# A two-layer hybrid trunk: where the constant tiles start, and corrections of attention scores over 64 or 128 rows of the array

## The chip, the cores and the metric

The kernel runs on one core of a Trainium2 chip. The metric is the time of one execution on the device in microseconds (us). Three runs of the kernel before gave 1586.66, 1589.82 and 1590.9 us; the median is 1589.82.

The engines of the core have short names in the profile: PE is TensorE's matmul, PEld its weight load, DVE is VectorE, ACT is ScalarE, POOL is GpSimd, SP is SyncE, which issues most of the transfers.

## The reference

Two layers over 512 positions of width 1024, all in float32. Each layer normalises x, projects it, mixes the positions in three ways side by side, adds the result to x, and then applies a gated feed-forward part with a short convolution. The part of the attention that the change touches:

```python
q = rmsnorm(da_q.reshape(B, S, DA_HEADS, 2, DA_QK_DIM), da_q_norm_g[l]) * (DA_QK_DIM ** -0.5)
k = rmsnorm(da_k.reshape(B, S, DA_HEADS, 2, DA_QK_DIM), da_k_norm_g[l])
...
s = jnp.einsum('bhmqd,bhmkd->bhmqk', qb, kh) + bias[None, :, None]
s = jnp.where(dist >= 0, s, neg)
p = jax.nn.softmax(s, axis=-1)
a = p[:, :, 0] - lam * p[:, :, 1]
return jnp.einsum('bhqk,bhke->bhqe', a, vh)
```

There are 4 heads, each with two maps (index m) of 64 features. The rest of a layer is retention over 4 heads, a short convolution, three gates of width 1024, an output projection, and the feed-forward part of width 2816.

## The kernel before, in words

**Exact products from two parts.** A float32 operand is held as two float32r tiles: the rounded value (hi) and what rounding left (lo). `mm3` (L145 to L149) multiplies hi by hi, hi by lo and lo by hi into one accumulator, so every product of the reference is three matmuls. The rows of the profile at L147, L148 and L149 are these three. `T.matmul(o, a, b)` lets `b` stream through the array while `a` stands in it as 128x128 weights; the profile names the streaming operand first.

**Work by position and by feature.** x lies transposed, in eight tiles of 128 features by 512 positions. `split_x` (L239) makes the two parts of each, times a gain. `natural` (L301) projects with x standing and the weights streaming, for what is wanted by position: the retention's queries, keys, values and gate (512 columns) and the heads (384 columns). `project` (L265) has the weights standing and x streaming, 512 columns: the convolution's inputs and gates (`proj_T`) and the feed-forward gate and up tiles (pg and pu). The branches (pb), the output projection (po) and the down projection (p2) stream other tiles: the mixers' outputs (om), the gated sum (y), the activations (act).

**Weights.** SyncE loads a weight tile, ScalarE rounds it (L138), VectorE subtracts (L139). Three pairs of these tiles take turns.

**The attention.** For each head `attention` (L425) turns queries and keys by transposes. Map m sits in rows 0 to 63 or 64 to 127. `qs2[:, m]` holds the hi part of a map's queries in the map's own half of the rows and the lo part in the other half; `kh2[:, m]` holds the hi part of the keys in both halves. One matmul over 128 rows (L462) gives hi times hi and lo times hi. What is missing, hi queries by lo keys, is the score correction (L465): the lo keys of both maps share one tile `kl` (L446, map 0 in its upper half, map 1 in its lower), and each correction is a matmul over the 64 rows of its map. A block of 128 queries has 128, 256, 384 or 512 keys, by the causal mask, so each head has four blocks with two maps: eight matmuls at L462 and eight at L465.

**Order.** `staggered` runs the heads and the retention in steps side by side, `weave` puts projections that do not depend on them between the steps, and a scheduler with its own estimate of durations settles the final order on each engine. On TensorE the two maps' matmuls of a block stand next to each other or with projection matmuls between them.

**Where tiles start.** A pool lays out its tiles one after the other in each partition, each rounded up to 32 bytes. The pool `cp` of constants comes first. It begins with two tiles of 512 bytes, a tile of 4 bytes (`warm`) and two of 560; x follows, 288 bytes past a multiple of 512, then the tables, then state, qz and the parts of x, all 480 bytes past a multiple of 512 (that is 32 past a multiple of 64). The pools `wp` (weights) and `tp` (om, y, act, queries, keys) come behind it, and in the kernel before their large tiles start on multiples of 2048.

Of the kernel before, what the change touches and what calls it, by code (L numbers as in the profile page):

```python
# [20 lines left out]
P = 128  # L21
D = 1024
S = 512
# [14 lines left out]
SINGLE = 1  # L38
SOME = 5
# [4 lines left out]
# columns of the packed per-layer parameters  # L44
# [5 lines left out]
def trunk(ctx, tc, xT, wr, wh, wt, wda, wret, wsc, wo, wf, w2, par, lamp, relb, onehot, mask, rope, gtab, out):  # L50
# [30 lines left out]
    def weave(first, second):  # L81
        """Steps of first, each followed by about COVER us of second."""
        due = 0.0
        for _ in first:
            due += COVER
            while due > 0.0:
                cost = next(second, None)
                if cost is None:
                    break
                due -= cost  # L90
        run(second)

    def staggered(tasks):
        """Tasks side by side, a step of each at a time, each from its own start on."""
        t = 0
        while tasks:
            live = []
            for start, task in tasks:
                if start <= t and next(task, DONE) is DONE:
                    continue  # L100
                live.append((start, task))
            tasks = live
            t += 1
            yield
# [12 lines left out]
    def ordered(i):  # L117
        """The program's first loads follow one another as they are written."""
        if starting[0]:
            tc.keep_in_program_order(i)  # L120
        return i
# [23 lines left out]
    def mm3(o, a, b, start, stop):  # L145
        """o += a.T @ b in float32, from operands in two exact parts."""
        T.matmul(o, a[0], b[0], start=start, stop=False)  # L147
        T.matmul(o, a[0], b[1], start=False, stop=False)  # L148
        T.matmul(o, a[1], b[0], start=False, stop=stop)  # L149

    def split(src, hi, lo, g=None):
        """float32 src (times a column) as two float32r parts."""
        if g is None:
            A.copy(hi, src)
            V.tensor_tensor(lo, src, hi.bitcast(F32), ALU.subtract)
        else:
            A.activation(hi, src, AF.Copy, scale=g)
            V.scalar_tensor_tensor(lo, src, g, hi.bitcast(F32), ALU.mult, ALU.subtract)
        return hi, lo
# [6 lines left out]
    ident = cp.tile([P, P], F32, name="ident")  # L166
    make_identity(nc, ident)
    ones = cp.tile([P, P], F32, name="ones")
    G.memset(ones, 1.0)
    warm = cp.tile([P, 1], F32, name="warm")  # L170
    A.activation(warm, ones[:, 0:1], AF.Tanh)
    # the array's clock rises with use: bring it up while the first loads are under way
# [7 lines left out]
    x = [cp.tile([P, S], F32, name=f"x{k}") for k in range(KT)]  # L180
# [5 lines left out]
    rope_t = cp.tile([P, 2, ST, 64], F32, name="rope_t")  # L186
    gtab_t = cp.tile([P, ST, 8], F32, name="gtab_t")
    mask_t = cp.tile([P, P], F32, name="mask_t")
    bias_t = cp.tile([P, H, S], F32, name="bias_t")
# [8 lines left out]
    def biases():  # L198
        """The negated relative bias, with the causal mask, as a Toeplitz tile per head."""
        rb = cp.tile([BUCKETS + 1, H], F32, name="rb")  # L200
        V.memset(rb[BUCKETS : BUCKETS + 1], -BIG)
        G.dma_start(rb[:BUCKETS], relb)
        line = dr.tile([H, 640], F32, name="line")
        for a, b in ((0, 512), (512, 640)):
            oh = temp(f"oh{a}", b - a)[: BUCKETS + 1]
            G.dma_start(oh, onehot[:, a:b])
            ps = aux(f"psb{a}")
            T.matmul(ps[:H, : b - a], rb, oh, start=True, stop=True)
            row = temp(f"line{a}", b - a)[:H]
            V.tensor_copy(row, ps[:H, : b - a])  # L210
            G.dma_start(line[:, a:b], row)
        skew = dr.tile([H, P * 640], F32, name="skew")
        G.dma_start(skew.rearrange("h (p n) -> h p n", n=640), line.unsqueeze(1).broadcast_to([H, P, 640]))
        src = skew[:, 127 : 127 + 639 * P].rearrange("h (p n) -> p h n", n=639)
        G.dma_start(bias_t, src[:, :, :S])

    # zero columns in front of what the convolutions read
# [4 lines left out]
    # the retention's states and queries of two heads, on the diagonal blocks  # L222
    state = cp.tile([P, 2, ST - 1, P], F32R, name="state")
    G.memset(state.bitcast(F32), 0.0)
    qz = [cp.tile([P, ST, 2, P], F32R, name=f"qz{a}") for a in range(2)]
# [3 lines left out]
    def rsqrt(f, v, n, name):  # L229
        """v ** -0.5: a first guess from the exponent, and Newton's steps to float32's last bit."""  # L230
        t = sp.tile([P, n], F32, tag=f"nt{n}", name=f"nt{name}", bufs=2)
        V.tensor_scalar(t.bitcast(I32), v.bitcast(I32), 1, None, ALU.logical_shift_right)
        V.tensor_scalar(f.bitcast(I32), t.bitcast(I32), -1.0, float(0x5F3759DF), ALU.mult, ALU.add)
        for _ in range(3):
            V.scalar_tensor_tensor(t, f, -0.5, f, ALU.mult, ALU.mult)
            V.tensor_tensor(t, t, v, ALU.mult)
            V.scalar_tensor_tensor(f, t, 1.5, f, ALU.add, ALU.mult)

    def split_x(l, which, name, k):  # L239
        """x times its gain in two parts."""  # L240
        hi = cp.tile([P, S], F32R, tag=f"xh{k}", name=f"xh{k}_{name}")
        lo = cp.tile([P, S], F32R, tag=f"xl{k}", name=f"xl{k}_{name}")
        return split(x[k], hi, lo, pars[l][:, which + k : which + k + 1])

    def norm_x(name):
        """1 / rms of x by column and by row."""
# [18 lines left out]
    def project(xg, ps, w):  # L265
        """ps[e, s] = sum over d of w[d, e] x[d, s], for 128 columns of a weight."""
        for k, xk in enumerate(xg):
            sl = slice(k * P, (k + 1) * P)
            mm3(ps, (w[0][:, sl], w[1][:, sl]), xk, k == 0, k == len(xg) - 1)

    def rms_cols(sq, n, scale, name):
        """(mean square + eps) ** -0.5 over the last axis of sq [p, n, d]."""
# [7 lines left out]
    def transposes(src, name):  # L280
        """Four 128 x 128 blocks of src(st), side by side in a bank."""
# [10 lines left out]
    def layer(l):  # L292
# [8 lines left out]
        def natural(src, w, name, evacuate):  # L301
            """w columns of the input projection by position, one bank per 128 positions; in steps."""
# [70 lines left out]
        # -lambda, in every partition  # L373
# [23 lines left out]
        def head_chunk(h):  # L397
            """Head h of the attention: queries and keys by position, values in two parts."""
# [26 lines left out]
        def attention(h):  # L425
            """A head in steps: scores and softmax of a block of queries, the difference of its two
            maps, its transpose, its product with the values; neighbouring blocks overlap."""
# [3 lines left out]
            # a map's queries in two parts above each other, against keys whose first part stands twice  # L431
# [3 lines left out]
            kl = tp.tile([P, S], F32R, tag="kl", name=f"kl{h}{L}", bufs=2)  # L435
# [6 lines left out]
            for m in range(2):  # L442
# [3 lines left out]
                V.scalar_tensor_tensor(kl[a], ps[a], gk[a], kh2[a, m].bitcast(F32), ALU.mult, ALU.subtract)  # L446
# [7 lines left out]
            def scores(i):  # L454
# [8 lines left out]
                for m in range(2):  # L463
                    # a map in either half of the array's rows
                    T.matmul(pS2[m][:, :W], qs2[halves[m], m, qs], kl[halves[m], :W], start=False, stop=True)  # L465
# [8 lines left out]
            def combine(i):  # L474
                # e0 / z0 - lambda e1 / z1, times z0
# [15 lines left out]
            def values(i):  # L491
                # against both parts of v at once, side by side
# [41 lines left out]
        kn = (wide(f"knh{L}"), wide(f"knl{L}"))  # L534

        def retention(p):
# [34 lines left out]
            def scores(b):  # L571
                # two blocks of positions, both heads
# [97 lines left out]
        def side(b, src, mats):  # L670
            """The gated sum over the short convolution (b = 2) and the retention (b = 1)."""
# [12 lines left out]
        # the retention and the heads, with what does not depend on them between their steps  # L684
# [73 lines left out]
def _consts():  # L758
    """Tables that depend on the shapes alone."""
# [18 lines left out]
    # the retention's decay between positions i and j, g ** i for queries, g ** -j / 8 for keys  # L778
# [11 lines left out]
def _layout(i):  # L790
    """The inputs as the program's tensors: tiles of weights that are contiguous by partition."""
    C = np.ascontiguousarray

    def cols(w, n):
        # [L, K*P, n*P] -> [L, n, P, K*P]
        L, kk, _ = w.shape
        return C(w.reshape(L, kk // P, P, n, P).transpose(0, 3, 2, 1, 4)).reshape(L, n, P, kk)
# [4 lines left out]
    def rows(w, n, width):  # L802
        # two rows of tiles beside each other
        return C(w.reshape(DEPTH, 4, 2, P, n, width).transpose(0, 4, 1, 3, 2, 5)).reshape(DEPTH, n, 4, P, 2 * width)

    def two(w):
        # two tiles of columns beside each other
# [53 lines left out]
```

## Time and profile before

| what | value |
|---|---|
| median of 3 runs | 1589.82 us (1586.66 to 1590.9) |
| span of the profiled execution | 1584.9 us |
| PE busy in it | 1577.1 us |
| DVE busy in it | 980.8 us |
| ACT busy in it | 627.1 us |
| granted TensorE clock | 1.000 |

The profile gives the span from the first to the last instruction of one execution; a run's time also holds the start and the end around it, so that the median of the runs lies 4.9 us above the span. A row of the timeline has the start, the time taken, the engine, the line, the operation and the tiles, out<-in. Matmuls are pipelined: their times overlap, so the distance from one start to the next tells what one costs in a stream.

### The profile page before, as it was taken

To read this page: it belongs to the slowest core of one execution; us is meant where nothing else is said; L and a number is where in the kernel's file an instruction comes from. 1 tells how busy PE (TensorE), PEld (TensorE's weight loads), DVE (VectorE), ACT (ScalarE), POOL (GpSimd) and SP (SyncE) were. 2 spreads that over 40 slices of the span, in tenths; PEclk is the share of its full clock that TensorE was granted. 3 is DMA by queue.
4 is the path that set the end of the run, shared out by engine and by line. 5 is a ranking of instruction groups with operands and counts; after the bars stand their busy time and mean duration, and the time that the engine had idled before them with its cause. 6 is when DMAs were issued, how large, how long until landed. Compare 5 with 4: busy or idle time off the path is not lost.

```text
span 1584.9 us, 18971 instructions
## 1 busy us (share of the span) xinstructions
PE 1577.1 (100%) x7286; PEld 1303.8 (82%) x7286; DVE 980.8 (62%) x1826; ACT 627.1 (40%) x1057; POOL 9.1 (1%) x21
## 2 busy tenths in 40 slices
PE   9999999999999999999999999999999999999998
PEld 7898887888888888888889988888888888888887
DVE  7488777554566456456656887765555763564562
ACT  4455664233333233233425565642333431332331
POOL 1000000000000000000000000000000000000000
PEclk9999999999999999999999999999999999999999
DMA  5322232232333332333322222322323333323323
GB/s 184 123 91 73 61 100 74 92 100 74 106 94 93 93 93 90 97 106 88 98 80 91 72 85 69 94 74 87 98 82 93 93 93 104 94 88 100 94 87 100
DMA packets 46891, 147.04 MB, mean 93 GB/s; under 512 B 6120, under 2 KB 6519, under 8 KB 46801
## 3 DMA queue, kind: packets, MB, share of 16 engines
q1 hardware_dynamic: 45216, 143.11, 30.2%
q0 software_dynamic: 1584, 2.72, 0.5%
q8 instruction: 57, 0.93, 0.3%
q14 instruction: 34, 0.27, 0.1%
HBM read 143.70 MB, written 3.42 MB: 93 GB/s over the span
## 4 chain that ended last, share of the span: by engine, by line
PE 98%; DMA 1%; DVE 0%; ACT 0%; issue 0%; SPq 0%; ACTq 0%; DVEq 0%
PE pnrvgL L147 1%; PE pnrvgL L149 1%; PE pnrvgL L148 1%; PE pnrqkL L148 1%; PE pnrqkL L149 1%; PE pnrqkL L147 1%; PE pnh3L L148 1%; PE pnh2L L149 1%; PE pnh3L L147 1%; PE pnh1L L147 1%; PE pnh2L L147 1%; PE pnh1L L148 1%; PE pnh1L L149 1%; PE pnh3L L149 1%; PE pnh2L L148 1%; PE pnh0L L147 1%
## 5 line engine op out<-in xcount | busy, mean ns | idle before, releaser
L138 ACT CAST hi_tL<-raw_tL 128x1024 fp32r<-128x1024 f32 x60 | 63.0, 1050 | 126.1 <-DMA raw_tL<-in_wt 21.8
L138 ACT CAST hi_fuL<-raw_fuL 128x1024 fp32r<-128x1024 f32 x44 | 46.3, 1052 | 156.1 <-issue 18.0
L138 ACT CAST hi_w2L<-raw_w2L 128x896 fp32r<-128x896 f32 (+1 forms) x48 | 47.1, 982 | 142.9 <-PE p200L L148 11.9
L139 DVE TENSOR_TENSOR lo_tL<-raw_tL,hi_tL 128x1024 fp32r<-128x1024 f32 x60 | 73.4, 1223 | 17.4 <-ACT hi_tL L138 17.0
L138 ACT CAST hi_fgL<-raw_fgL 128x1024 fp32r<-128x1024 f32 x44 | 46.3, 1053 | 83.8 <-issue 13.0
L139 DVE TENSOR_TENSOR lo_fuL<-raw_fuL,hi_fuL 128x1024 fp32r<-128x1024 f32 x44 | 53.9, 1225 | 27.4 <-ACT hi_fuL L138 27.4
L139 DVE TENSOR_TENSOR lo_w2L<-raw_w2L,hi_w2L 128x896 fp32r<-128x896 f32 (+1 forms) x48 | 54.4, 1133 | 3.9 <-ACT hi_w2L L138 2.3
L139 DVE TENSOR_TENSOR lo_fgL<-raw_fgL,hi_fgL 128x1024 fp32r<-128x1024 f32 x44 | 53.6, 1219 | 3.5 <-ACT hi_fgL L138 3.5
L138 ACT CAST hi_oL<-raw_oL 128x1024 fp32r<-128x1024 f32 x16 | 16.9, 1053 | 57.2 <-PE ptg7L L148 13.4
L148 PE MATMUL pnrqkL<-lo_nrqkL,xh_mL 128*128 128x512 f32 x64 | 25.6, 400 | 0.1
L149 PE MATMUL pnrvgL<-hi_nrvgL,xl_mL 128*128 128x512 f32 x64 | 25.4, 397 | 0.0
L148 PE MATMUL pnrvgL<-lo_nrvgL,xh_mL 128*128 128x512 f32 x64 | 25.4, 396 | 0.0
L149 PE MATMUL pnrqkL<-hi_nrqkL,xl_mL 128*128 128x512 f32 x64 | 25.1, 395 | 0.0
L147 PE MATMUL pnrqkL<-hi_nrqkL,xh_mL 128*128 128x512 f32 x64 | 23.7, 405 | 1.0 <-ACT hi_nrqkL L138 1.0
L147 PE MATMUL pnrvgL<-hi_nrvgL,xh_mL 128*128 128x512 f32 x64 | 24.1, 399 | 0.0
L149 PE MATMUL pnh2L<-hi_nh2L,xl_mL 128*128 128x384 f32 x64 | 22.3, 349 | 0.0
L148 PE MATMUL pnh3L<-lo_nh3L,xh_mL 128*128 128x384 f32 x64 | 22.2, 347 | 0.0
L147 PE MATMUL pnh3L<-hi_nh3L,xh_mL 128*128 128x384 f32 x64 | 22.2, 347 | 0.0
L139 DVE TENSOR_TENSOR lo_oL<-raw_oL,hi_oL 128x1024 fp32r<-128x1024 f32 x16 | 19.6, 1225 | 4.1 <-ACT hi_oL L138 4.1
L147 PE MATMUL pnh1L<-hi_nh1L,xh_mL 128*128 128x384 f32 x64 | 21.8, 341 | 0.0
L147 PE MATMUL pnh2L<-hi_nh2L,xh_mL 128*128 128x384 f32 x64 | 21.8, 340 | 0.0
L148 PE MATMUL pnh1L<-lo_nh1L,xh_mL 128*128 128x384 f32 x64 | 21.8, 340 | 0.0
(3622 smaller groups left out, 5046.7 us busy)
## 6 DMA issues: line engine op xcount, KB each, us to landing
raw_tL<-in_wt SPq DMA_DIRECT2D x60, 512.0 KB, 3.6
raw_fgL<-in_wf SPq DMA_DIRECT2D x44, 512.0 KB, 3.5
raw_fuL<-in_wf SPq DMA_DIRECT2D x44, 512.0 KB, 3.6
raw_w2L<-in_w SPq DMA_DIRECT2D x32, 448.0 KB, 3.3
raw_oL<-in_wo SPq DMA_DIRECT2D x16, 512.0 KB, 3.6
raw_w2L<-in_w SPq DMA_DIRECT2D x16, 512.0 KB, 3.5
raw_nrvgL<-in_wr SPq DMA_DIRECT2D x8, 512.0 KB, 3.6
raw_bdL<-in_wda SPq DMA_DIRECT2D x16, 256.0 KB, 2.6
```

The lines of the kernel that those rows point to most:

```text
L138: A.copy(hi, raw)
L139: V.tensor_tensor(lo, raw, hi.bitcast(F32), ALU.subtract)
L147: T.matmul(o, a[0], b[0], start=start, stop=False)
L148: T.matmul(o, a[0], b[1], start=False, stop=False)
L149: T.matmul(o, a[1], b[0], start=False, stop=stop)
```

## The change

Three things are done.

1. The tiles of the pool `cp` stand in another order, behind a tile of 96 floats that nobody uses. x, the parts of x, the new keys, state, qz, two tables and the biases all start on multiples of 512 bytes. `warm` and `rb` are made wider than what is used of them. The pools behind `cp` move with it: weights and activations start on multiples of 512, at 512 bytes past a multiple of 2048; the parts of x start 1536 past one.
2. The two parts of an x tile are one tile `xs` with two halves, where they were two tiles. It is kept through the program.
3. The lo keys of the two maps stand in `klz`, a constant tile with one half for each map: map 0's keys over zeros, map 1's under zeros. The zeros are written once at the start by POOL. The score correction is a matmul over all 128 rows: hi queries by lo keys, plus lo queries by zeros. There is one such tile for all heads, where two tiles `kl` took turns.

Comments are also taken out, which moves the line numbers: L462 and L465 of before are L465 and L466 of the changed kernel.

```diff
+FILL = 96
...
     ident = cp.tile([P, P], F32, name="ident")
+    ones = cp.tile([P, P], F32, name="ones")
+    cp.tile([P, FILL], F32, name="fill")
+    x = [cp.tile([P, S], F32, name=f"x{k}") for k in range(KT)]
+    xs = [cp.tile([P, 2, S], F32R, name=f"xs{k}") for k in range(KT)]
+    klz = cp.tile([P, 2, S], F32R, name="klz")
+    state = cp.tile([P, 2, ST - 1, P], F32R, name="state")
+    qz = [cp.tile([P, ST, 2, P], F32R, name=f"qz{a}") for a in range(2)]
+    rope_t = cp.tile([P, 2, ST, 64], F32, name="rope_t")
+    mask_t = cp.tile([P, P], F32, name="mask_t")
+    bias_t = cp.tile([P, H, S], F32, name="bias_t")
     make_identity(nc, ident)
-    ones = cp.tile([P, P], F32, name="ones")
     G.memset(ones, 1.0)
-    warm = cp.tile([P, 1], F32, name="warm")
-    A.activation(warm, ones[:, 0:1], AF.Tanh)
...
+    warm = cp.tile([P, 32], F32, name="warm")
+    A.activation(warm[:, 0:1], ones[:, 0:1], AF.Tanh)
...
-        rb = cp.tile([BUCKETS + 1, H], F32, name="rb")
+        rb = cp.tile([BUCKETS + 1, 16], F32, name="rb")[:, :H]
...
-    state = cp.tile([P, 2, ST - 1, P], F32R, name="state")
     G.memset(state.bitcast(F32), 0.0)
-    qz = [cp.tile([P, ST, 2, P], F32R, name=f"qz{a}") for a in range(2)]
+
+    G.memset(klz.bitcast(F32), 0.0)
     for t in qz:
         G.memset(t.bitcast(F32), 0.0)
...
     def split_x(l, which, name, k):
-        hi = cp.tile([P, S], F32R, tag=f"xh{k}", name=f"xh{k}_{name}")
-        lo = cp.tile([P, S], F32R, tag=f"xl{k}", name=f"xl{k}_{name}")
-        return split(x[k], hi, lo, pars[l][:, which + k : which + k + 1])
+        return split2(x[k], xs[k], pars[l][:, which + k : which + k + 1])
...
-            kl = tp.tile([P, S], F32R, tag="kl", name=f"kl{h}{L}", bufs=2)
...
-                V.scalar_tensor_tensor(kl[a], ps[a], gk[a], kh2[a, m].bitcast(F32), ALU.mult, ALU.subtract)
+                V.scalar_tensor_tensor(klz[a, m], ps[a], gk[a], kh2[a, m].bitcast(F32), ALU.mult, ALU.subtract)
...
-                for m in range(2):
-                    # a map in either half of the array's rows
-                    T.matmul(pS2[m][:, :W], qs2[halves[m], m, qs], kl[halves[m], :W], start=False, stop=True)
+                    T.matmul(pS2[m][:, :W], qs2[:, m, qs], klz[:, m, :W], start=False, stop=True)
```

On TensorE the order changes where the corrections stand. In the first head of the first layer, block 1 of the queries (pS0 and pS1 are the two maps' scores, k0 and q0 keys and queries), before:

```order
L149 MATMUL por11L_1125<-state,rT1L_818 128x2x64
L462 MATMUL pS001L_1199<-k0L_972,q0L_971 128x256
L462 MATMUL pS101L_1200<-k0L_972,q0L_971 128x256
L465 MATMUL pS001L_1199<-kl0L_973,q0L_971 128x256
L465 MATMUL pS101L_1200<-kl0L_973,q0L_971 128x256
L488 MATMUL pT00L_1213<-ident,s000L_1080 128x128
```

and in the changed kernel:

```order
L150 MATMUL por11L_1119<-state,rT1L_813 128x2x64
L465 MATMUL pS001L_1193<-k0L_967,q0L_966 128x256
L466 MATMUL pS001L_1193<-klz,q0L_966 128x256
L465 MATMUL pS101L_1194<-k0L_967,q0L_966 128x256
L466 MATMUL pS101L_1194<-klz,q0L_966 128x256
L489 MATMUL pT00L_1207<-ident,s000L_1074 128x128
```

A map's correction now follows its own first matmul; the two corrections no longer stand next to each other.

The scheduler also moves some blocks between other matmuls. In the second head, block 3 (pS013, pS113) stood between a gate's projection (ptg17) and a branch (pb12), before:

```order
L149 MATMUL ptg17L_1884<-xh_mL_229,lo_tL_1881 128x512
L462 MATMUL pS013L_1912<-k1L_1456,q1L_1455 128x512
L465 MATMUL pS013L_1912<-kl1L_1457,q1L_1455 128x512
L462 MATMUL pS113L_1913<-k1L_1456,q1L_1455 128x512
L465 MATMUL pS113L_1913<-kl1L_1457,q1L_1455 128x512
L147 MATMUL pb12L_1971<-oms0L_1033,hi_b2L_1865 128x512
```

and in the changed kernel it stands behind that branch, in the next gate's projection (ptg18):

```order
L148 MATMUL ptg18L_1978<-xs_86,hi_tL_1974 128x512
L465 MATMUL pS013L_1905<-k1L_1450,q1L_1449 128x512
L466 MATMUL pS013L_1905<-klz,q1L_1449 128x512
L149 MATMUL ptg18L_1978<-xs_86,hi_tL_1974 128x512
L465 MATMUL pS113L_1906<-k1L_1450,q1L_1449 128x512
L466 MATMUL pS113L_1906<-klz,q1L_1449 128x512
L150 MATMUL ptg18L_1978<-xs_86,lo_tL_1975 128x512
```

The block comes seven matmuls later in the program's order, and a projection matmul stands between its maps.

More of the change, by code (lines that the diff above doesn't have):

```diff
@@ L179, in trunk @@
         ordered(nc.sync.dma_start(pars[0], par[0]))
-    x = [cp.tile([P, S], F32, name=f"x{k}") for k in range(KT)]
     def load_x(k):
@@ L184, in load_x @@
             ordered(nc.sync.dma_start(x[k], xT[:, k]))
-    rope_t = cp.tile([P, 2, ST, 64], F32, name="rope_t")
     gtab_t = cp.tile([P, ST, 8], F32, name="gtab_t")
-    mask_t = cp.tile([P, P], F32, name="mask_t")
-    bias_t = cp.tile([P, H, S], F32, name="bias_t")
     def constants():
```

## The prediction

> **What bounds the kernel now.** I read the page first, then who waited for TensorE, then the stretches of two stages, then single matmuls in order of time.
>
> ```profile
> span 1584.9 us, 18971 instructions
> PE 1577.1 (100%) x7286; PEld 1303.8 (82%) x7286; DVE 980.8 (62%) x1826; ACT 627.1 (40%) x1057; POOL 9.1 (1%) x21
> ```
>
> TensorE has work in flight all the time, and the next engine is busy for 62%. The waits of TensorE say whether anybody holds it up:
>
> ```profile
> PE por00L L594 <- ACT PT00L L154: 1.6, 1, 1.6
> PE pnrqkL L147 <- ACT hi_nrqkL L138: 1.0, 1, 1.0
> ```
>
> Its longest waits after the first microseconds come to 2.6 us of 1584.9. So the time is the number of matmuls times the distance from the start of one to the start of the next (I call it the step; the durations overlap and are no measure). A change pays where it shortens steps, and only there. The two halves of an FFN group, as stretches from their first matmul to the first of what follows (columns: stretch, length, then busy time and count by engine, clock, DMA):
>
> ```profile
> 563.24:641.64 78.40, 78.40 (x338) 63.12 (x336) 48.52 (x61) 27.72 (x34) 0.00 (x0) 1.00 0.30 91
> 641.64:679.74 38.10, 38.10 (x169) 31.54 (x168) 15.55 (x18) 8.44 (x10) 0.00 (x0) 1.00 0.34 99
> ```
>
> Taking the weight loads as the count, gate and up projections run at 78.40 / 336 = 233.3 ns a step, the down projection at 38.10 / 168 = 226.8 ns. Both stream 512 columns against 128x128 weights at clock 1.00, and neither waits. They differ in what streams: the parts of x, which start 480 bytes past a multiple of 512 (32 past one of 64), against the activations, which start on a multiple of 2048. The input projection by position has the roles turned, misplaced x standing and well placed weights streaming:
>
> ```profile
> 817.64 0.39 PE L149 MATMUL pnrqkL<-hi_nrqkL,xl_mL 128*128 128x512 f32 x1
> ...
> 819.98 0.40 PE L147 MATMUL pnrvgL<-hi_nrvgL,xh_mL 128*128 128x512 f32 x1
> 843.42 0.33 PE L148 MATMUL pnh0L<-lo_nh0L,xh_mL 128*128 128x384 f32 x1
> ...
> 855.73 0.28 PE L557 MATMUL pR00L<-rv0L,knhL 128*128 128x256 f32 x1
> ```
>
> Ten steps of 512 columns take 2.34 us, 234 ns each: a misplaced operand costs the same on either side. Between the other two rows lie 71 steps of 384 columns in 12.31 us, 173.4 ns each.
>
> **Part 1, placement.** All parts of x move to multiples of 512. Matmuls of 512 columns that stream x: 44 FFN tiles, 24 gates and 6 convolution tiles of 24 matmuls, two layers: 3552. At 233.3 - 226.8 = 6.5 ns each: 23.1 us. Those with x standing: 384, at 234 - 226.8 = 7.2 ns: 2.8 us. The four heads have 768 of 384 columns, of which no well placed run exists; the bounds are 0 (nothing left to gain) and 768 x 6.5 ns = 5.0 us (the same gain as at 512 columns). I take 2.5, the middle, since both ends are equally far. Where a well placed tile follows x, the first steps are still long:
>
> ```profile
> 303.13 0.39 PE L147 MATMUL pb51L<-omr0L,hi_b1L 128*128 128x512 f32 x1
> ...
> 304.52 0.40 PE L147 MATMUL ptg14L<-xh_mL,hi_tL 128*128 128x512 f32 x1
> ```
>
> Six steps in 1.39 us are 0.03 us over 6 x 226.8 ns; there are 48 such places: 1.4 us. Placement: 23.1 + 2.8 + 2.5 + 1.4 = 29.8 us. Every one of these steps is on the path, since TensorE waits for nobody in these stages.
>
> [...]
>
> **Part 2, score corrections.** One head of the attention, its four blocks of queries (L462 over 128 rows, L465 over 64):
>
> ```profile
> 153.56 0.22 PE L462 MATMUL pS010L<-k1L,q1L 128*128 128x128 f32 x1
> 153.71 0.33 PE L465 MATMUL pS010L<-kl1L,q1L 64*128 64x128 f32 x1
> 153.97 0.45 PE L147 MATMUL pnh2L<-hi_nh2L,xh_mL 128*128 128x384 f32 x1
> 154.25 0.34 PE L148 MATMUL pnh2L<-lo_nh2L,xh_mL 128*128 128x384 f32 x1
> 158.41 0.33 PE L462 MATMUL pS011L<-k1L,q1L 128*128 128x256 f32 x1
> 158.59 0.28 PE L462 MATMUL pS111L<-k1L,q1L 128*128 128x256 f32 x1
> 158.79 0.38 PE L465 MATMUL pS011L<-kl1L,q1L 64*128 64x256 f32 x1
> 158.80 0.38 PE L465 MATMUL pS111L<-kl1L,q1L 64*128 64x256 f32 x1
> 159.11 0.45 PE L149 MATMUL pnh2L<-hi_nh2L,xl_mL 128*128 128x384 f32 x1
> 159.39 0.33 PE L147 MATMUL pnh2L<-hi_nh2L,xh_mL 128*128 128x384 f32 x1
> 173.00 0.42 PE L462 MATMUL pS012L<-k1L,q1L 128*128 128x384 f32 x1
> ...
> 173.90 0.50 PE L148 MATMUL ptg17L<-xl_mL,hi_tL 128*128 128x512 f32 x1
> 174.24 0.40 PE L149 MATMUL ptg17L<-xh_mL,lo_tL 128*128 128x512 f32 x1
> 179.59 0.40 PE L462 MATMUL pS013L<-k1L,q1L 128*128 128x512 f32 x1
> 179.91 0.49 PE L465 MATMUL pS013L<-kl1L,q1L 64*128 64x512 f32 x1
> 180.33 0.50 PE L462 MATMUL pS113L<-k1L,q1L 128*128 128x512 f32 x1
> 180.77 0.50 PE L465 MATMUL pS113L<-kl1L,q1L 64*128 64x512 f32 x1
> 181.19 0.50 PE L147 MATMUL pb12L<-oms0L,hi_b2L 128*128 128x512 f32 x1
> 181.53 0.39 PE L148 MATMUL pb12L<-oms0L,hi_b2L 128*128 128x512 f32 x1
> ```
>
> A step into the 64-row form and a step out of it are long: 512 columns take 0.32 and 0.42 us where 0.227 is usual, and the matmul behind steps 0.28 instead of 0.173, or 0.34 instead of 0.23: 0.107 us each time. Two 64-row matmuls that stand side by side do start together (158.79, 158.80), but the pair then takes 0.31 us. Sum for this head: the block of 128 columns twice 0.41, 256 columns 0.70, 384 columns 0.90, 512 columns 1.60, five followers 0.53: 4.55 us; eight heads over two layers: 36.4 us.
>
> After the change all four matmuls of a block use 128 rows. Their steps by the nearest rows: 0.227 and 0.173 from above; shorter ones from the retention:
>
> ```profile
> 856.65 0.28 PE L149 MATMUL pS00L<-qz,rT2L 128*128 128x256 f32 x1
> 856.77 0.28 PE L147 MATMUL pS00L<-qz,rT2L 128*128 128x256 f32 x1
> 108.88 0.27 PE L148 MATMUL por10L<-state,rT1L 128*128 128x128 f32 x1
> 108.99 0.27 PE L149 MATMUL por10L<-state,rT1L 128*128 128x128 f32 x1
> ```
>
> 0.12 and 0.11. A head is 4 x (0.227 + 0.173 + 0.12 + 0.11) = 2.52 us, eight 20.2 us: 16.2 us less. I take 16, since the scheduler pairs the other heads' corrections a little better. Bounds: 13 if each block keeps one long follower (32 x 0.107 us = 3.4 us), 18 if the 128-column step falls to 0.06.
>
> [...]
>
> **Part 3, what else moves.** The corrections' keys are now one tile for all heads, where two took turns. The next head's write must follow the last read:
>
> ```profile
> 140.51 0.50 PE L465 MATMUL pS103L<-kl0L,q0L 64*128 64x512 f32 x1
> 148.50 0.74 DVE L446 SCALAR_TENSOR_TENSOR kl1L<-pt11L,par,k1L 64x512 fp32r<-64x512 f32 x1
> ```
>
> The read ends at 141.0, the write begins at 148.5 behind transposes that TensorE issues later still: 7.5 us of cover, cost 0. Were it gone, VectorE would stand with the weight splits queued behind the write, and TensorE after them. The zero half is one more memset on POOL, like those of qz:
>
> ```profile
> 2.10 1.83 POOL L227 MEMSET qz<- 128x1024 f32 x2
> ...
> 34.23 0.54 POOL L206 DMA_DIRECT2D oh<-in_onehot  x1 [29.68 <-DVE tb1L L345]
> ```
>
> Two of them take 1.83 us, so one more takes 0.9; POOL then idles for 29.7 us, and this hides it (0.9 us if it did not). Steps moved between other matmuls in the attention stage change no sum. Against the gain, TensorE at the start and at the 1.6 us wait for PT00 is released by loads and splits that do not get faster: I give back 0.6 us.
>
> **Sum.** 29.8 + 16.0 - 0.6 = 45.2 us. The profiled span goes from 1584.9 to 1539.7; the runs' median, 1589.8, lies 4.9 above that span: **1544.6 us**.
>
> **Rivals.**
> (a) The start is not the cause: x is slow because of where its pool lies or what it is used with. For it: no tile of x has been seen elsewhere. Against: the same 7 ns whether x streams or stands. Then only part 2 counts: 1589.8 - 16 = 1573.8. [...]
> (b) The long steps belong to the corrections as such, and the full form keeps half: 1552.6.
> [...]
> (d) The slower side: what counts is a start on 2048 bytes. Before, the weights and activations had it, x not; now x, weights and activations are all 512 or 1536 past one. If each misplaced operand costs 6.5 ns, the 3936 matmuls of 512 columns with x go up by 6.5 and the 1824 without by 13: 25.6 + 23.7 = 49.3 us, less 16: 1623. It decides against the change from 2.1 ns per operand (16 x 6.5 / 49.3). For it: every fast moving tile of 512 columns starts on 2048. Against: a head's weights stream alternately from 0 and 1536 past 2048, and the 71 steps above stay at 173.4 ns.
>
> **How the numbers follow.** Forecast 0.82, (a) 0.06, (b) 0.05, (c) 0.03, (d) 0.04. The forecast's own range is 1539 to 1551: 2.5 either way for the heads, 3 for the corrections, 2 for reordered waits. The range over all cases goes up to 1556, which takes in (b) and some stall at the single tile, and down to 1537. A measurement of this kernel tells about 0.3%, 4.8 us, from no change: faster 0.95, same 0.01, slower 0.04.
>
> **What will show it.** Gate and up projections at 226.8 ns a step like the down projection (right), at 233 (rival a), both at 233 or more (d). The corrections with 128 rows and steps no longer than the ones before them, and the matmul behind them back at 0.17 or 0.23. VectorE waiting for TensorE at the corrections' write would show the single tile as a cost. A wait of TensorE above 2 us anywhere makes the sum wrong.

## The result, and the profile after

The changed kernel takes 1548.87 us in the median of 4 runs (1548.07 to 1551.65), the kernel before 1589.99 (1586.66 to 1590.9): a ratio of 0.9754, 95% interval 0.9739 to 0.9770. That is 41 us by the two medians and 39 us by the ratio. The predicted time was 1544.6.

The page of the changed kernel, and its waits of TensorE:

```profile
span 1546.0 us, 18968 instructions
PE 1538.0 (99%) x7286; PEld 1304.6 (84%) x7286; DVE 980.2 (63%) x1826; ACT 625.3 (40%) x1057; POOL 10.0 (1%) x22
```

```profile
PE por00L L595 <- ACT PT00L L155: 1.8, 1, 1.8
PE pnrqkL L148 <- ACT hi_nrqkL L139: 0.9, 1, 0.9
```

As many matmuls as before, nearly the same two waits (2.6 us before, 2.7 now), and 38.9 us less span: the gain lies in shorter steps, not in waits. The stretches of the same feed-forward group as before (gate and up projections, then the down projection):

```profile
548.32:624.48 76.16, 76.16 (x338) 63.06 (x336) 48.55 (x61) 27.73 (x34) 0.00 (x0) 1.00 0.30 94
624.48:662.56 38.08, 38.08 (x170) 31.53 (x168) 15.56 (x18) 8.44 (x10) 0.00 (x0) 1.00 0.33 100
```

Both now run at 226.7 ns a step (76.16 / 336 and 38.08 / 168); the down projection had that before, the gate and up projections had 233.3. Single matmuls of the changed kernel in order of time, for the score blocks of one head (L465 is the first matmul of a map, L466 its correction, now with 128 rows), for a head's projection, and for the projection by position:

```profile
149.99 0.33 PE L150 MATMUL pnh2L<-hi_nh2L,xs 128*128 128x384 f32 x1
150.16 0.22 PE L465 MATMUL pS010L<-k1L,q1L 128*128 128x128 f32 x1
150.22 0.27 PE L466 MATMUL pS010L<-klz,q1L 128*128 128x128 f32 x1
150.34 0.39 PE L148 MATMUL pnh2L<-hi_nh2L,xs 128*128 128x384 f32 x1
150.56 0.33 PE L149 MATMUL pnh2L<-lo_nh2L,xs 128*128 128x384 f32 x1
...
154.47 0.34 PE L465 MATMUL pS011L<-k1L,q1L 128*128 128x256 f32 x1
154.64 0.28 PE L466 MATMUL pS011L<-klz,q1L 128*128 128x256 f32 x1
154.76 0.28 PE L465 MATMUL pS111L<-k1L,q1L 128*128 128x256 f32 x1
154.88 0.28 PE L466 MATMUL pS111L<-klz,q1L 128*128 128x256 f32 x1
155.00 0.34 PE L150 MATMUL pnh2L<-hi_nh2L,xs 128*128 128x384 f32 x1
...
177.29 0.39 PE L465 MATMUL pS113L<-k1L,q1L 128*128 128x512 f32 x1
177.52 0.39 PE L466 MATMUL pS113L<-klz,q1L 128*128 128x512 f32 x1
177.75 0.39 PE L150 MATMUL ptg18L<-xs,lo_tL 128*128 128x512 f32 x1
...
797.69 0.40 PE L150 MATMUL pnrqkL<-hi_nrqkL,xs 128*128 128x512 f32 x1
...
799.98 0.39 PE L148 MATMUL pnrvgL<-hi_nrvgL,xs 128*128 128x512 f32 x1
...
822.93 0.34 PE L149 MATMUL pnh0L<-lo_nh0L,xs 128*128 128x384 f32 x1
...
835.24 0.28 PE L558 MATMUL pR00L<-rv0L,knhL 128*128 128x256 f32 x1
```

A map's two matmuls of 128 keys take 0.18 us, of 256 keys 0.24 once the block runs, of 512 keys 0.46. No step of a correction is more than 0.01 us longer than the usual step of its width: its medians are 0.11, 0.12, 0.18 and 0.23 us at 128, 256, 384 and 512 columns, where before the longest were 0.26, 0.31, 0.37 and 0.43. The ten steps with x standing take 2.29 us where they took 2.34. The 71 steps of a head's projection take 12.31 us, to the hundredth what they took before.

The steps of each group, added up over the span from start to start (us; the matmul that follows a score block counts with its own group):

| steps | before | after | difference |
|---|---|---|---|
| gate and up tiles, 2112 | 493.1 | 479.25 | -13.85 |
| gates of the branches, 1152 | 271.6 | 263.8 | -7.8 |
| convolution inputs, 288 | 68.4 | 66.6 | -1.8 |
| x standing, 512 columns, 384 | 92.6 | 90.4 | -2.2 |
| heads, 384 columns, 768 | 137.2 | 136.05 | -1.1 |
| branches, output and down projection and the attention's second product | 433.4 | 431.2 | -2.2 |
| scores and corrections | 31.3 | 20.9 | -10.4 |
| all the rest | 57.3 | 57.8 | +0.5 |

### The profile page after: what moved, and what is told of

It is laid out like the page before. It is cut to its first block, busy times and chain, and to the rows that moved or that the text cites. A ratio compares the mean times of both kernels' runs of the same rounds, so it can differ in the third digit from the quotient of the medians.

```text
span 1546.0 us, 18968 instructions
## 1 busy us (share of the span) xinstructions
PE 1538.0 (99%) x7286; PEld 1304.6 (84%) x7286; DVE 980.2 (63%) x1826; ACT 625.3 (40%) x1057; POOL 10.0 (1%) x22
## 4 chain that ended last, share of the span: by engine, by line
PE 98%; DMA 1%; DVE 0%; ACT 0%; issue 0%; SPq 0%; ACTq 0%; DVEq 0%
PE pnrvgL L150 1%; PE pnrvgL L148 1%; PE pnrvgL L149 1%; PE pnrqkL L149 1%; PE pnrqkL L150 1%; PE pnrqkL L148 1%; PE pnh3L L149 1%; PE pnh1L L148 1%; PE pnh2L L150 1%; PE pnh3L L148 1%; PE pnh2L L148 1%; PE pnh1L L150 1%; PE pnh2L L149 1%; PE pnh1L L149 1%; PE pnh3L L150 1%; PE pnh0L L148 1%
## 5 line engine op out<-in xcount | busy, mean ns | idle before, releaser
L149 PE MATMUL pnrqkL<-lo_nrqkL,xs 128*128 128x512 f32 x64 | 25.2, 394 | 0.1
L150 PE MATMUL pnrvgL<-hi_nrvgL,xs 128*128 128x512 f32 x64 | 25.1, 392 | 0.0
L149 PE MATMUL pnrvgL<-lo_nrvgL,xs 128*128 128x512 f32 x64 | 25.0, 391 | 0.0
L150 PE MATMUL pnrqkL<-hi_nrqkL,xs 128*128 128x512 f32 x64 | 24.8, 390 | 0.0
L159 DVE SCALAR_TENSOR_TENSOR xs<-x,par,xs 128x512 fp32r<-128x512 f32 x32 | 23.9, 746 | 1.1 <-ACT xs L158 1.1
L148 PE MATMUL pnrqkL<-hi_nrqkL,xs 128*128 128x512 f32 x64 | 23.5, 403 | 0.9 <-ACT hi_nrqkL L139 0.9
L158 ACT ACTIVATE xs<-x,par 128x512 fp32r<-128x512 f32 x32 | 23.0, 718 | 3.0 <-DMA x<-in_xT 3.0
L148 PE MATMUL pnrvgL<-hi_nrvgL,xs 128*128 128x512 f32 x64 | 23.7, 394 | 0.0
L149 PE MATMUL pnh3L<-lo_nh3L,xs 128*128 128x384 f32 x64 | 22.1, 346 | 0.0
L150 PE MATMUL pnh2L<-hi_nh2L,xs 128*128 128x384 f32 x64 | 21.9, 343 | 0.0
L149 PE MATMUL pnh2L<-lo_nh2L,xs 128*128 128x384 f32 x64 | 21.7, 339 | 0.0
L148 PE MATMUL pnh1L<-hi_nh1L,xs 128*128 128x384 f32 x64 | 21.7, 338 | 0.0
```

## Experiments

Two questions were open. Do the two halves of the change add up, each with its own part of the gain? And is it the start of a tile that makes a step long, as the prediction had it, or something else that moved with it? All kernels were compared with the kernel before on the same chip (medians 1586.59 to 1587.13 us).

### Each half alone

Only the new layout, with the old corrections of 64 rows and their two tiles `kl`:

```diff
-    klz = cp.tile([P, 2, S], F32R, name="klz")
...
+            kl = tp.tile([P, S], F32R, tag="kl", name=f"kl{h}{L}", bufs=2)
...
-                    T.matmul(pS2[m][:, :W], qs2[:, m, qs], klz[:, m, :W], start=False, stop=True)
+                for m in range(2):
+                    T.matmul(pS2[m][:, :W], qs2[halves[m], m, qs], kl[halves[m], :W], start=False, stop=True)
```

> The new starts of the tiles with the old corrections over 64 rows (lo keys of both maps in one tile that takes turns). My theory: start and corrections are two separate gains. All 512-column steps fall to 226.7 ns, the 384-column ones stay at 173.4, the scores' matmuls keep their 31.3 us and the matmul behind them its extra 0.107 us; about 25 us faster than before, 1565 us. Rival (the placement has no worth of its own, for instance because x is slow by the use it is put to): 1590 us, steps of x at 233.

Only the corrections over 128 rows, in the layout of before:

```diff
+    klz = cp.tile([P, 2, S], F32R, name="klz")
+    G.memset(klz.bitcast(F32), 0.0)
...
-                    T.matmul(pS2[m][:, :W], qs2[halves[m], m, qs], kl[halves[m], :W], start=False, stop=True)
+                    T.matmul(pS2[m][:, :W], qs2[:, m, qs], klz[:, m, :W], start=False, stop=True)
```

> The old starts of the tiles with the corrections over 128 rows (new tile of lo keys beside zeros, 480 bytes past a multiple of 512). My theory: the scores' matmuls fall from 31.3 to about 21 us and the matmuls behind them lose most of their 5 us: 14 us faster than before, 1576 us; x steps stay at 233. Rival (two 64-row matmuls at once are worth keeping): 1590 us or slower. Rival (the two parts of the change need each other): the two runs' gains do not add up to the 41 us of the whole change.

The layout alone: 1564.24 us, ratio 0.9854 (0.9839 to 0.9869). The rows alone: 1572.13 us, 0.9905 (0.9888 to 0.9921). The product of the two ratios is 0.9760; the whole change has 0.9754. So they add up: some 23 us belong to the layout, some 15 to the rows. Three of the four executions of the layout alone had a mean granted clock below 1.000 (0.997 to 0.999; the last section looks into one of them); the fourth took 1562.02 us at 1.000, so the layout may be worth up to 25 us. In the timeline of the layout alone the old form of the corrections is still there, with its cost:

```profile
158.05 0.34 PE L464 MATMUL pS011L<-k1L,q1L 128*128 128x256 f32 x1
158.22 0.28 PE L464 MATMUL pS111L<-k1L,q1L 128*128 128x256 f32 x1
158.43 0.38 PE L466 MATMUL pS011L<-kl1L,q1L 64*128 64x256 f32 x1
158.44 0.38 PE L466 MATMUL pS111L<-kl1L,q1L 64*128 64x256 f32 x1
158.75 0.44 PE L150 MATMUL pnh2L<-hi_nh2L,xs 128*128 128x384 f32 x1
```

The pair of corrections takes 0.32 us from 158.43 to the next start at 158.75, and the step into it is 0.21 us; in the changed kernel (154.47 to 155.00) the whole block takes 0.53, here 0.70, as in the kernel before with its other layout (158.41 to 159.11). Where x lies has no part in it.

### What the corrections cost

The changed kernel without L466. The product of hi queries and lo keys is left out of the scores.

```diff
-                    T.matmul(pS2[m][:, :W], qs2[:, m, qs], kh2[:, m, :W], start=True, stop=False)
-                    T.matmul(pS2[m][:, :W], qs2[:, m, qs], klz[:, m, :W], start=False, stop=True)
+                    T.matmul(pS2[m][:, :W], qs2[:, m, qs], kh2[:, m, :W], start=True, stop=True)
```

> The changed kernel without its score corrections: hi queries by lo keys is left out. Sixty-four matmuls of 128 rows fewer. At the steps of the first half of each block (0.227, 0.173, 0.12 and 0.11 us, twice for each of eight heads) they are worth 10.1 us: 1539. If the long steps belong to the corrections as such and the full form kept half of them, it is 18 or more: 1531 or less. If their time was hidden beside other matmuls: 1549.

1537.79 us, ratio 0.9693 (0.9677 to 0.9709). Against it the corrections cost 11.1 us with 128 rows (1548.87; the spans say 10.5) and 26.5 us with 64 rows (1564.24, the layout alone; 24.2 by its execution at the full clock). Sixty-four matmuls over half the rows cost 2.2 to 2.4 times as much as the same over all rows, half of them zeros. The 10.1 expected for the full form was close, so it keeps none of the long steps. The same place as above, in the timeline without corrections:

```profile
151.29 0.22 PE L465 MATMUL pS010L<-k1L,q1L 128*128 128x128 f32 x1
151.35 0.39 PE L148 MATMUL pnh2L<-hi_nh2L,xs 128*128 128x384 f32 x1
151.58 0.33 PE L149 MATMUL pnh2L<-lo_nh2L,xs 128*128 128x384 f32 x1
```

The matmul behind a block of 128 columns takes 0.23 us without a correction, too (0.22 at 150.34 with one). What is left of a long follower there is not the correction's.

### The start, or the distance between the two operands

Two kernels move tiles by less than 512 bytes. In the first the parts of x lie 64 bytes further (x itself, which TensorE does not read, stays); in the second the filler in front is 32 bytes longer, so that all tiles behind it lie 32 bytes past a multiple of 512, the streaming and the standing ones. Of what TensorE reads, only `ident` and `ones` lie ahead of the filler and stay.

```diff
     x = [cp.tile([P, S], F32, name=f"x{k}") for k in range(KT)]
+    cp.tile([P, 16], F32, name="front")
     xs = [cp.tile([P, 2, S], F32R, name=f"xs{k}") for k in range(KT)]
+    cp.tile([P, 112], F32, name="behind")
```

> The changed kernel with the parts of x alone moved by 64 bytes (a filler before them and one behind, all other tiles where the change has them). If a start on a multiple of 64 bytes is all that counts, x steps stay at 227 ns and the time at 1549 us. If the boundary is 128 bytes or more (512 as the change chose), x steps go to 233 ns in 3936 matmuls: 26 us slower, 1575 us.

```diff
-FILL = 96
+FILL = 104
```

> The changed kernel with its first filler 32 bytes longer, so that every tile starts 32 bytes past a multiple of 512: now the streaming and the standing operand are both misplaced, which no matmul of 512 columns was before. If each misplaced operand costs its own 6.6 ns, all 5760 steps of 512 columns go to 240 ns: 76 us slower than the changed kernel, 1625 us. If one misplaced operand costs what two cost, they go to 233.4 ns: 38 us slower, 1587 us. If only the distance between the two operands counts (both now equally off), they stay at 227: 1549 us.

All tiles 32 bytes off: 1548.04 us, ratio 0.9754 (0.9740 to 0.9769), the time of the changed kernel. Only the parts of x 64 bytes off: 1562.14 us, 0.9839 (0.9825 to 0.9854), between the two times that were expected. Stretches of the same group, first with all tiles 32 bytes off, then with the parts of x 64 bytes off:

```profile
548.15:624.31 76.16, 76.16 (x338) 63.09 (x336) 48.55 (x61) 27.73 (x34) 0.00 (x0) 1.00 0.30 94
624.31:662.39 38.08, 38.08 (x170) 31.54 (x168) 15.55 (x18) 8.44 (x10) 0.00 (x0) 1.00 0.34 101
```

```profile
554.74:631.67 76.93, 76.93 (x338) 63.13 (x336) 48.54 (x61) 27.73 (x34) 0.00 (x0) 1.00 0.30 93
631.67:669.80 38.13, 38.13 (x170) 31.55 (x169) 15.55 (x18) 8.45 (x10) 0.00 (x0) 1.00 0.33 102
```

With all these starts off a multiple of 64 the steps are as short as they get, 226.7 ns. So the start is not the cause. With x at a distance of 64 bytes from the weights, gate and up steps are 228.9 ns: two thirds of the cost are gone. With x standing the distance has the other sign, -64, and the median step is 234 ns: no gain there. What counts is the distance between the two operands of a matmul, and the next kernels try which distances.

### Which distances cost

The parts of x are moved against the weights by one amount, om, y and act by another (with a filler pool ahead of theirs, which moves everything in that pool, queries and keys too). The diff is that of the first, 128 bytes for x and 96 for the others (32 and 24 floats); the second has 256 and 192, the third 160 and 224:

```diff
+    gp = ctx.enter_context(tc.tile_pool(name="gp", bufs=1))
+    gp.tile([P, 24], F32, name="gap")
     tp = ctx.enter_context(tc.tile_pool(name="tp", bufs=1))
...
     x = [cp.tile([P, S], F32, name=f"x{k}") for k in range(KT)]
+    cp.tile([P, 32], F32, name="front")
     xs = [cp.tile([P, 2, S], F32R, name=f"xs{k}") for k in range(KT)]
+    cp.tile([P, 96], F32, name="behind")
```

> The changed kernel with the parts of x 128 bytes later and om, y and act 96 bytes later than a multiple of 512, weights as they were. If every distance between the streaming and the standing operand other than a multiple of 512 costs: gate and up projections above 228 ns a step (x streams, distance 128), down projection above 228 (distance 96), and at 6.5 ns each 3936 and 1824 steps give 1549 + 25.6 + 11.9 = 1586. If the cost comes back with a period of 128 bytes: gate and up projections at 226.8, down projection at up to 233, at most 1549 + 11.9 = 1561. If what counts is the start of an operand on 64 bytes: gate and up at 226.8, down at 233, the same 1561.

> The changed kernel with the parts of x 256 bytes later and om, y and act 192 bytes later. If every distance other than a multiple of 512 costs: both projections of a feed-forward group above 228 ns a step, up to 1586. With a period of 256 or 128 bytes: gate and up at 226.8, down above, at most 1561. If the start on 64 bytes is what counts: both at 226.8, 1549.

> The changed kernel with the parts of x 160 bytes later and om, y and act 224 bytes later. Every theory of the distance has both projections above 226.8: at 233 each 1586, at 229 each 1549 + 5760 x 2.2 ns = 1562. If a distance other than 0 is the cheapest, one of these three kernels should show a projection below 226 ns a step.

One execution each: 1584.58 (granted clock 0.999), 1560.38 and 1587.65 us. The stretches of the group in the three kernels, in this order:

```profile
560.49:638.89 78.40, 78.40 (x338) 63.07 (x336) 48.56 (x61) 27.69 (x34) 0.00 (x0) 1.00 0.30 91
638.89:678.10 39.21, 39.21 (x170) 31.54 (x168) 15.56 (x18) 8.41 (x10) 0.00 (x0) 1.00 0.32 100
```

```profile
552.20:628.38 76.18, 76.18 (x337) 63.09 (x336) 48.56 (x61) 27.74 (x34) 0.00 (x0) 1.00 0.31 94
628.38:667.58 39.20, 39.20 (x169) 31.44 (x168) 15.55 (x18) 8.40 (x10) 0.00 (x0) 1.00 0.33 100
```

```profile
560.64:639.35 78.71, 78.71 (x337) 63.33 (x336) 48.55 (x61) 27.73 (x34) 0.00 (x0) 1.00 0.30 91
639.35:678.55 39.20, 39.20 (x169) 31.61 (x168) 15.56 (x18) 8.41 (x10) 0.00 (x0) 1.00 0.33 99
```

The down projection, untouched by all that is done to x, is now slow as soon as act is moved: 233.3 ns and more. At 256 bytes the gate and up projections are back at 226.7. Two more kernels move the parts of x alone (with the lines `front` and `behind` as above), by 256 and by 32 bytes.

> The changed kernel with only x and the parts of x 256 bytes later. If the step repeats every 256 bytes of distance: all steps of 512 columns at 226.8, 1549, no difference to the changed kernel. If the start on 512 or the distance modulo 512 counted: 1549 + 3936 x 6.5 ns = 1575.

> The changed kernel with only x and the parts of x 32 bytes later, so x streams at a distance of +32, where the kernel before has it at -32. If both signs cost the same: gate and up projections at 233 ns, 1549 + 3936 x 6.5 ns = 1575. If +32 is a cheap distance, as +64 with 229 ns is half cheap: 1549 to 1558.

At 256 bytes: 1548.47 us, ratio 0.9761 (0.9739 to 0.9782), as the changed kernel. At 32 bytes: 1572.55 us in one execution, and the gate and up stretch:

```profile
555.67:634.07 78.40, 78.40 (x337) 62.97 (x336) 48.53 (x61) 27.71 (x34) 0.00 (x0) 1.00 0.30 91
```

All multiples of 32 bytes below 256 are thus measured. Steps of 512 columns, streaming minus standing operand, modulo 256 (a stretch's length by 336 or 168):

| distance in bytes | 0 | 32 | 64 | 96 | 128 | 160 | 192 | 224 |
|---|---|---|---|---|---|---|---|---|
| ns a step | 226.7 | 233.3 | 228.9 | 233.4 | 233.3 | 234.3 | 233.3 | 233.3 |

The period of 256 is shown at two places: at 0 (226.7 ns at 256 as well) and at 224 (233.3 ns; the kernel before, with x streaming at 480, has 233.3 too). Each stretch is from one execution and has 168 or 336 steps. The projections by position, where x stands and the sign turns round, agree: the median step within a product is 227 ns at 0 and 232 to 234 ns at 32, 96, 128, 192 and 224. No distance that was tried gave less than the 226.7 ns of 0, and no layout that was tried beat the changed kernel's.

### Whose standing operand

In the changed kernel's trace the weights of the next matmul are loaded while one streams: the load for the L148 that starts at 138.89 takes 0.19 us from 138.66, where the L150 ahead of it starts. To tell a matmul's own weights from the next one's, only the lo weights are moved by 128 bytes; one product's three matmuls then have distances 0, 0 and 128, and x, om, y and act lie as in the changed kernel.

```diff
+            hi = wp.tile([P, n], F32R, tag="hi" + tag, name=f"hi_{name}", padded_shape=[P, pad], bufs=bufs)
+            if new:
+                wp.tile([P, 32], F32, tag="ahead" + tag, name="ahead" + tag, bufs=1)
+            lo = wp.tile([P, n], F32R, tag="lo" + tag, name=f"lo_{name}", padded_shape=[P, pad], bufs=bufs)
+            if new:
+                wp.tile([P, 32], F32, tag="behind" + tag, name="behind" + tag, bufs=1)
```

> The changed kernel with only the lo weight tiles 128 bytes later; x, the hi weights, om, y and act stay on multiples of 512. Of the three matmuls of a product in gate, up and down projections, the first two have hi weights standing, the third lo weights (distance 128 to what streams). If a matmul's own standing operand counts, the steps from the third one's start are at 232 ns and the others at 226.8. If the weights that are loaded for the next matmul while this one streams count, the steps from the second one's start are at 232. If both do, both. A third of 5760 steps at 5 ns more: 1549 + 10 = 1559 for one of the two, 1568 for both. If the starts of x and hi alone set it: 1549.

1571.46 us in one execution. The group's stretches:

```profile
555.10:632.75 77.65, 77.65 (x337) 63.53 (x336) 48.55 (x61) 27.73 (x34) 0.00 (x0) 1.00 0.30 92
632.75:671.58 38.83, 38.83 (x170) 31.77 (x168) 15.56 (x18) 8.43 (x10) 0.00 (x0) 1.00 0.33 101
```

Against 76.16 the gate and up stretch is 1.49 us longer, 13.3 ns for each of its 112 products: two steps of 6.6 ns too long, where one matmul of three has a bad distance. Taken apart by the matmul that they start from, the steps of the down projections are 226.7, 232.5 and 234.2 ns (means of 346, 346 and 292 steps): the third is slow, which has the moved weights, and so is the second, which streams ahead of it. Both count, the third expectation. The time is 3.5 us above its 1568, mainly because a slow step costs some 6.6 ns where the expectation took 5; the projections by position, in which the lo weights stream at 128 bytes, add only 0.6 us to what they took in the changed kernel.

## Why the prediction was right, and where not

**What bounds the kernel** held: TensorE busy for 99%, the same waits, each saved step taken off the span.

**Part 1, its cause.** The step that fails is "a misplaced operand": that starts off a multiple of 512 make steps long. With all starts 32 bytes off, the steps stay at 226.7 ns, and x 256 bytes past a multiple of 512 costs nothing. What the prediction saw as a misplaced x was x at a bad distance from the weights, 480 bytes, and the change set it to 0. The observation that the cost is the same on either side (233.3 ns a step with x streaming, 234 with x standing) fitted both readings and should have been a hint: one tile off is the same mismatch whichever of the two it is. The prediction's profile held no stretch in which both operands were off by the same amount, so it could not tell the two apart. The time came out right on this point by luck: the change puts all tiles at one place, and there both readings say the same. For all tiles 32 bytes off they do not, and there a price for each misplaced operand gave 1625 us where 1548.04 were measured.

**Part 1, its size.** Predicted 29.8, measured about 23 to 25. The largest term was right: 6.5 ns for each of 2112 gate and up steps are 13.7 us, measured 13.85. Too high were these:
- The heads' 768 steps of 384 columns, 2.5 us as the middle between two bounds: 0. Their steady step is 173.4 ns before and after, and the layout alone takes 0.24 us from them. The upper bound carried a price from 512 columns to 384, where the median steps differ by 2 ns (175 before, 173 after).
- The gates of the branches, 1152 x 6.5 = 7.5 us: 6.0 in the layout alone. Before, all but 10 of these steps took 228 ns or more, so the price was there; but with the new layout 328 of 1152 still do. These steps stand between score blocks and other narrower matmuls, and behind those a step is not short at once (228 to 233 ns in the mean for the second to the tenth, as the last section shows). The price came from a stretch without such neighbours.
- Branches behind x, 1.4 us: 0.8. x standing, 2.8: 2.7, as predicted. Of the two measured figures the 23 holds the lower clock (0.997 to 0.999) in three executions of the layout alone, the 25 is free of it.

**Part 2.** Predicted 16.0, measured 14.6 by the medians of the rows alone. The blocks themselves gave 10.4 us of it (31.3 to 20.9), where the working had 12.0 (32.2 and 20.2): one head stood for all, and a block's first matmul can still be followed by a long step (0.27 us at 169.63, 384 columns behind transposes of 128). The rest is the followers. They were to fall by 0.107 us each, and the ones behind blocks of 256, 384 and 512 columns did. Behind 128 columns the next 384 columns keep 0.23 us where 0.173 is usual, which the run without corrections has too; but there the block's first step is 0.06 where the working had 0.11, so this adds next to nothing.

**Part 3** held. The single tile of the corrections' keys stalls nobody. VectorE's wait list for the writes of klz names only ScalarE, and POOL's new memset ends long before POOL's next wait:

```profile
its engine sat idle before it (us, times) until:
  ACT k2L L448: 1.9, 2
  ACT k3L L448: 1.9, 4
```

```profile
2.10 0.94 POOL L231 MEMSET klz<- 128x1024 f32 x1
...
34.13 0.54 POOL L212 DMA_DIRECT2D oh<-in_onehot  x1 [28.68 <-DVE tb1L L349]
```

**The sum.** The span was to fall by 45.2 us to 1539.7 and fell by 38.9 to 1546.0: 6.3 too much. The other way, the prediction added 4.9 us to the span, the median of three runs less the span of the profiled one. The profiled execution of the changed kernel took 1548.07 us, 2.1 around its span, and the kernel before had medians of 1586.6 to 1587.1 in the later comparisons: of the 4.9 us, more than half was scatter between its executions. The two errors have opposite signs, and a part of the good agreement is that.

**The rivals.** (a) had the right sentence, that the start is not the cause and that it matters what x is used with, and the wrong consequence: the placement was not worth 0 but 23 us. (b) is out by the run without corrections: 10.5 to 11.1 us for them, the price of usual steps. (c), at 0.03, has two 64-row matmuls at once as the form worth keeping. No run shows a saving by them: the form with 64 rows costs 24 to 26.5 us, the form with 128 rows 11.1; the pair at 158.43 starts together and still takes 0.32 us, where two full steps of 256 columns take 0.24. (d) is out by the changed kernel itself: its weights and activations start 512 bytes past a multiple of 2048, and the down projection stays at 226.7 ns.

## What to carry to other kernels

When TensorE is the bound, divide a stretch without waits by its number of matmuls and compare stretches of the same width: a few ns between them that no wait explains are worth a look at where both operands lie, here at their distance modulo 256 bytes (226.7 ns at 0, 233.3 at 224). Do not count on the full gain where the stream is broken up: here the gates' steps, between narrower matmuls, gained 6.0 us instead of 7.5. Before a cause is named, ask which layouts the profile has not shown; a single kernel with both operands moved by the same amount told the start from the distance (all tiles 32 bytes off: 1548.04 us). And half-height matmuls between full-height ones were dearer here than full-height ones over zeros (24 to 26.5 us against 11.1), by the long step in and the long follower. Last, look at the granted clock of every run before a difference of 2 us is explained: the layout alone took 1562.02 us at 1.000 and 1564.01 at 0.999.

## What the runs showed of the hardware that was not expected

- The step of 512 columns in float32r went with the distance between what streams and what stands: 226.7 ns at 0 and at 256 bytes, 228.9 at 64, 233.3 to 234.3 at six others below 256. The weights that are loaded for the next matmul count as well as a matmul's own: with the lo weights alone 128 bytes off, the three steps of a product are 226.7, 232.5 and 234.2 ns. At 384 columns there is little of it: 173.4 ns for 71 steps at 0 and at 32 (the kernel before), and medians over all heads of 173 ns at 0 and 175 at 32. Why 64 alone is cheaper, and why a step is not shorter than 226.7, no run here tells.
- The short step comes only after a while. At distance 0 in the changed kernel:

```profile
161.03 0.39 PE L148 MATMUL ptg16L<-xs,hi_tL 128*128 128x512 f32 x1
...
163.11 0.39 PE L148 MATMUL ptg16L<-xs,hi_tL 128*128 128x512 f32 x1
...
164.47 0.28 PE L501 MATMUL po01L<-v1L,aT10L 128*128 128x256 f32 x1
```

  Behind matmuls of 384 columns, nine steps take 2.08 us, 231 ns each; the next six take 1.36 us, 227 ns each. Over the whole trace, the second to the tenth step of 512 columns behind a narrower matmul have means of 228 to 233 ns, and the eleventh to the thirteenth of 226.6 to 226.8 (steps that end at a narrower matmul are left out). So the table above holds for streams that have run on for some ten steps; why they need them, no run here tells.
- A wait can cost more than its length. In four of the thirteen profiled executions the mean granted clock is 0.998 or 0.999: in the layout alone, in the rows alone, in the kernel with 128 and 96 bytes, and with the parts of x 64 bytes off. In the layout alone TensorE waits 2.0 us for PT00 until 76.12 us, and the clock is at 0.50 from 76.08 for 3.41 us; worked out from these two figures, that costs another 1.7 us. In the rows alone, behind a wait of 1.8 us for PT00, the stretch from 76 to 82 us has a mean clock of 0.72, which comes to the same 1.7. The changed kernel waits 1.8 us there as well and keeps 1.00. Stretches of 3.41 us, laid so that the clock's changes fall on their borders, show a difference. First the layout alone, then the kernel with 256 and 192 bytes, then the changed kernel (the second number behind the stretch is the time for which TensorE is busy, the third from last the granted clock):

```profile
72.66:76.08 3.42, 1.45 (x11) 1.24 (x9) 2.49 (x6) 2.88 (x8) 0.80 (x1) 1.00 0.23 37
76.08:79.49 3.41, 3.37 (x13) 3.08 (x14) 3.35 (x11) 3.36 (x10) 0.00 (x0) 0.50 0.91 347
...
72.85:76.26 3.41, 1.65 (x12) 1.44 (x10) 2.39 (x5) 2.87 (x8) 0.80 (x1) 1.00 0.29 51
76.26:79.67 3.41, 3.27 (x23) 3.06 (x24) 3.35 (x10) 3.36 (x11) 0.00 (x0) 1.00 0.97 387
...
71.74:75.15 3.41, 2.84 (x19) 2.63 (x17) 1.28 (x2) 2.33 (x6) 0.80 (x1) 1.00 0.15 60
75.15:78.56 3.41, 2.17 (x15) 1.99 (x16) 3.41 (x11) 2.85 (x10) 0.00 (x0) 1.00 0.79 260
```

  Behind the stretch with 1.45 us of TensorE at work, 42% of it, the clock is at half; behind those with 1.65 us and more it stays. In the kernel before, the stretch from 74.86 to 78.27 us has 1.84 us, and the clock stays too. In the changed kernel a border falls into the wait of 1.8 us, and the stretches on both sides keep 2.84 and 2.17 us of work. Executions of one kernel differ by it as well: three of the four of the layout alone have a clock of 0.997 to 0.999 and take 1564.01 to 1565.36 us, the fourth has 1.000 and takes 1562.02. What sets the clock beyond this, no run here tells.
- Narrow matmuls pass time on to the next one: after two steps of 128 columns of 0.06 and 0.11 us, or after a single one of 0.06, the step of the next 384 columns is 0.23 us instead of 0.173. The sum is nearly that of steps of 0.11, 0.11 and 0.173.
